# Reordering conv-out's seven products, metering the convolution's work, and beginning the first FFN in another order, in a two-layer decoder kernel

## The chip, the cores and the metric

One core of one Trainium2 chip runs the whole program. The metric is device time in microseconds (us), the median of several runs. TensorE is PE in the profile, VectorE DVE, ScalarE ACT, GpSimd POOL and SyncE SP.

## What is computed

The reference is a decoder of two layers in fp32, with D = 1024, S = 1024 tokens and d_ff = 2816. Layer 0 mixes tokens by a short gated convolution, layer 1 by dilated attention. Each mixer and each FFN is added to a residual stream behind an RMSNorm, and a last norm ends it:

```python
def short_conv_mixer(h, w_in, conv_k, w_out):
    b, c, u = jnp.split(h @ w_in, 3, axis=-1)
    y = lax.conv_general_dilated(c * u, conv_k[:, None, :], window_strides=(1,),
        padding=[(CONV_WIDTH - 1, 0)], dimension_numbers=("NWC", "WIO", "NWC"),
        feature_group_count=D_MODEL)          # depthwise, causal, width 3
    return (b * y) @ w_out
# x = x + mixer(rms_norm(x));  x = x + (silu(h @ w_gate) * (h @ w_up)) @ w_down, h = rms_norm(x)
```

## The kernel before

**Products.** Activations lie transposed: 8 tiles X[n] of 128 features by 1024 tokens, used as two halves of 512 columns. Each fp32 matrix product is made of three fp32r matmuls, since each operand is split into a high part (ACT, L159 for weights, L605 for moving operands) and a low part, the rest (DVE, L160 and L606). On top of that, `Strassen` multiplies 2x2 blocks with Winograd's seven products, numbered 1 to 7. Some take a difference or sum of weight blocks (the `combo` tiles, L227) or of moving blocks (t2, t3, `sums`). A whole product is twelve matmuls of 128x512: four tiles of the inner dimension, for each high by high (L613), high by low (L614) and low by high (L615). Its result is accumulated in one of 8 PSUM banks, used in rotation. The results of one bank are copied by ACT (`save`, L619) or added by DVE (`add`, L623).

**Order.** All instructions are written out in program order, each engine runs its own in that order, and waits follow from the data. `unit_order` gives the order of pairs (u, m) in a stage, where u is a unit (a pair of blocks of weight rows) and m the product. The weights of the coming products are loaded by SP into `raw` tiles and split ahead of use; how far ahead is set by tables (`upto`, `ahead`, AHEAD) and by calls of `ensure`. The hooks `start`, `filled` and `entry` are called behind each product and place everything else.

**The convolution layer.** `Conv` runs the in-projection in 12 units: unit u belongs to group q = u // 3, and u % 3 says whether its result is the c gate, the value or the b gate. For every result the generator `work` is put at the end of the list `waiting`. It multiplies c by the token's 1/rms (L1045), the value by c (L1049), runs the taps (`conv`: four instructions of 480, 32, 448 and 64 columns at L1034 and a multiply by 1/rms at L1035), multiplies by the b gate (L1057) and stores. `step(upto)` moves the list on by so much work: `idle` calls step(2) behind each product of the in-projection, `drain` calls step(4) or step(1) behind those of conv-out. `store` makes the differences that conv-out's products need (L787, L789) and sends all blocks to DRAM by POOL, except those of the last group, the `near` pair, that stay in SBUF.

**Conv-out.** `down` runs the products in the order DOWN = 1, 2, 6, 7, 4, 5, 3, each for four pairs k = 0, 2, 4, 6 of output tiles: 28 products. I write "product m of pair k". `feed` brings moving operands: SP loads blocks from DRAM (`hin`) and they are split; it is stepped behind products, and earlier at the products listed in CONV_FEED. Every product's result is copied or added into X (L858, L860), and the residual comes by an accumulating transfer from POOL (L850). The hook `entry` then squares finished halves of X for the FFN's norm (`chained`, L489: the third and fourth reach their sums by an accumulating transfer, later ones by DVE adds at L490), splits the sum of squares (ACT L516, DVE L520), sums over features by matmuls with ones (L528) and makes 1/rms with a logarithm and an exponential on ACT (L529, L530). The FFN's first eight moving operands are `first_half`: scale X (hcol, L1303), then split (L605, L606). The other column half comes in `second_half`, from tiles that `gained` made (ACT, and an accumulating transfer).

**First FFN and attention.** The FFN (`Swiglu`, stage key 0) starts with the products (0,1), (1,1), (0,2), (1,2), (2,1). Behind the first of them, `start(0)` runs `last_step` and the second half's statistics. In the attention layer, `QueryKey.mix` makes the operands of its first products (`differences`, L983 and L984) and has the statistics' copies and low parts made in the hook behind product (1,2), their ones-matmuls behind (3,1).

Of the kernel before, what the change touches and what calls it, by code (L numbers as in the profile page):

```python
# [13 lines left out]
ALU = mybir.AluOpType  # L14
# [101 lines left out]
def trunk(ctx: ExitStack, tc: tile.TileContext, x, gains_in, cwi, ck, cwo, wqkv, wo, relb,  # L116
# [103 lines left out]
    def add_pair(u, rows, w, eng, upto, low=(), sub=ALU.subtract):  # L220
# [13 lines left out]
        def summed(m):  # L234
            if m not in t:
                if m == 7:
                    t[7] = combo(raw(7, 0, 0), raw(7, 1, 0), sub)
                elif m == 3:
                    t[3] = combo(raw(3, 0, 1), t[6], sub)
                else:  # L240
                    t[5] = combo(raw(6, 1, 0), raw(6, 1, 1), ALU.add)
                    t[6] = combo(t[5], raw(6, 0, 0), sub)
            return t[m]

        def part(m):
            if m in (1, 2, 4):
                src = raw(m, *{1: (0, 0), 2: (0, 1), 4: (1, 1)}[m])
            else:
                src = summed(m) if m == 6 else (summed(m), t.pop(m))[0]
# [3 lines left out]
        sums_of.update({("m", u, m): lambda m=m: summed(m) for m in (6, 7, 3)})  # L253
# [44 lines left out]
    def unit_order(nu, conv):  # L298

        order = [(0, 1), (1, 1), (0, 2), (1, 2), (2, 1), (2, 2), (3, 1)]  # L300
# [3 lines left out]
        else:  # L304
            order += [(3, 2)] + [(u, m) for m in (6, 7, 4, 5) for u in (0, 1)]
            order += [(2, 6), (0, 3), (1, 3), (2, 5), (2, 7)]
            order += [(3, 6), (2, 4), (2, 3), (3, 5), (3, 7), (4, 1), (3, 4), (3, 3)]
# [7 lines left out]
        u = nu - 1  # L315
        return order[:-1] + [(u, 6), (u, 5), (u, 7), (u - 1, 3), (u, 4), (u, 3)]

    def add_units(key, nu, column):

        early = key in (CONV, QK)  # L320
        units, slabs, base = [], {}, len(raw_src)
        raw_base[key] = base
        for u in range(nu):
            if early:

                rows = ((0, 1), (2, 6), (3, 7, 8), (4, 9, 10), (5, 11, 12))[u] if u < 5 else (2 * u + 3, 2 * u + 4)
            else:
                rows = ((0, 1), (2, 5), (3, 6), (4, 7))[u] if u < 4 else (2 * u, 2 * u + 1)
            for n in range(len(rows)):
                slabs[rows[n]] = column(u, n % 2)  # L330
            if early:
# [3 lines left out]
                ahead.update({m: 6 if u < 5 else 2 * u + 6 for m in (1, 2)})  # L335
            elif u < 4:
# [14 lines left out]
            if not early and u > 4 and u % 2:  # L351
                add_deep(units[u], key, u, [[base + r - 2 * (1 - v) for r in rows] for v in range(2)],
                         lambda i, u=u: base + 2 * u + {1: 1, 2: 1, 3: 3, 4: 3}.get(i, 2))
        raw_src.extend(slabs[r] for r in range(len(slabs)))
        ops.extend(units[u][m] for u, m in unit_order(nu, early))
# [5 lines left out]
    def add_down(i, w):  # L361

        at = 0
        for c, qs in enumerate(chunks[CONV] if i == CONV else laid):
# [5 lines left out]
            upto = lambda m, r, u: r + {1: 4 + u, 2: 7, 5: 8 + u, 3: 11}.get(m, 7)  # L370
            units = [add_pair((i, c, 2 * u), (r + u, r + 4 + u), span, nc.vector,
                              lambda m, r=r, u=u: upto(m, r, u), sub=ALU.add) for u in range(4)]
# [1765 lines left out]
```

## Time and profile before

| | us |
|---|---|
| median of 3 runs (2090.3 to 2091.05) | 2090.67 |
| the profiled execution | 2091.3 |
| its span | 2089.5 |
| PE busy | 2066.4 |
| DVE busy | 1780.6 |
| ACT busy | 1052.9 |
| POOL busy | 283.9 |

The profiled execution took 1.8 us more than its span, and 0.6 more than the median. Times in rows are from the start of the span. A row of a timeline gives the start, the length, engine, line, operation, tiles out<-in, their shapes, and in brackets the idle time before it with what ended it. A row of the waits gives the waiter, what it waited for, the microseconds in total, how often, and the longest. A row of the windows gives a stretch and its length, busy time and count of each engine, the mean granted clock of PE (1.00 is full), and the share and rate of the DMA engines. In-projection ends at 242.29, conv-out at 328.94. A matmul's shown length is modelled and overlaps the next; matmuls are counted by their pitch, from start to start.

### The profile page before, as it was taken

Reading aid. Unit: us, or ns where it says so; the run is one execution under the profiler, and the core shown is the slowest. Engines: PE = TensorE matmul, PEld = TensorE weight load, DVE = VectorE, ACT = ScalarE, POOL = GpSimd, SP = SyncE. Lnnn points to the kernel's source line nnn. Section 1 sums busy time; section 2 is a strip of 40 time slices with the busy share of each in tenths; the row PEclk is TensorE's granted clock in tenths of the full one; section 3 lists DMA queues with packets and bytes.
Section 4 is the critical chain, followed back from the end, with each engine's and each line's share of the span. In section 5 each row is a group of like instructions: output and inputs, shape, how many; then the busy total and the mean of one; then the engine's idle time right before and its main releaser. Section 6 shows DMA issues by size and latency. Waiting matters only on the chain.

```text
span 2089.5 us, 30878 instructions
## 1 busy us (share of the span) xinstructions
PE 2066.4 (99%) x10906; PEld 1779.3 (85%) x10906; DVE 1780.6 (85%) x3318; ACT 1052.9 (50%) x1978; POOL 283.9 (14%) x398
## 2 busy tenths in 40 slices
PE   9999999999999999999999999999999999999998
PEld 7888787888888888887889999998888888888887
DVE  8898979988888888798985888988998888887896
ACT  7433466444443454456544666665544434455443
POOL 1000111110110111010223333311011001002000
PEclk9999999999999999999999999999999999999999
DMA  7223573233233488543656867955222333368532
GB/s 220 98 96 106 172 206 81 101 104 99 106 104 109 148 245 216 177 114 128 225 194 200 213 166 216 247 180 154 71 95 103 107 103 109 111 204 230 161 101 81
DMA packets 136201, 308.31 MB, mean 148 GB/s; under 512 B 15868, under 2 KB 46670, under 8 KB 136048
## 3 DMA queue, kind: packets, MB, share of 16 engines
q1 hardware_dynamic: 96272, 201.67, 31.9%
q0 software_dynamic: 32144, 89.98, 14.6%
q10 hardware_dynamic: 7632, 14.70, 1.9%
q8 instruction: 86, 1.41, 0.3%
q14 instruction: 67, 0.55, 0.1%
HBM read 211.30 MB, written 85.81 MB: 142 GB/s over the span
## 4 chain that ended last, share of the span: by engine, by line
PE 52%; DVE 1%; ACT 0%; issue 0%; DVEq 0%
PE bank L615 10%; PE bank L613 10%; PE bank L614 10%; PE bank L1732 5%; PE bank L415 2%; PE bank L417 2%; PE bank L416 2%; PE bank L1601 2%; PE bank L1603 1%; PE bank L1602 1%; PE bank L708 1%; PE bank L707 1%; PE bank L705 1%; PE bank L1658 1%; PE bank L1657 1%; DVE x L2047 0%
## 5 line engine op out<-in xcount | busy, mean ns | idle before, releaser
L614 PE MATMUL bank<-b,w 128*128 128x512 f32 x2176 | 850.2, 391 | 7.8 <-DVE b L606 7.5
L613 PE MATMUL bank<-b,w 128*128 128x512 f32 x2176 | 849.8, 391 | 1.8 <-ACT w L159 1.8
L615 PE MATMUL bank<-b,w 128*128 128x512 f32 x2176 | 849.4, 390 | 1.8 <-DVE w L160 1.7
L614 PEld LDWEIGHTS bank<-b,w 128*128 128x128 f32 x2176 | 409.8, 188 | 94.0 <-DVE b L606 9.6
L615 PEld LDWEIGHTS bank<-b,w 128*128 128x128 f32 x2176 | 409.7, 188 | 89.3 <-DVE w L160 4.2
L613 PEld LDWEIGHTS bank<-b,w 128*128 128x128 f32 x2176 | 410.1, 188 | 87.1 <-ACT w L159 2.5
L159 ACT ACTIVATE w<-combo 128x512 fp32r<-128x512 f32 (+2 forms) x512 | 268.9, 551 | 281.0 <-DVE combo L227 239.7
L160 DVE TENSOR_TENSOR w<-combo,w 128x512 fp32r<-128x512 f32 (+2 forms) x512 | 297.7, 594 | 34.2 <-ACT w L159 33.6
L619 ACT ACTIVATE part<-bank 128x512 f32<-128x512 f32 x192 | 114.5, 596 | 390.3 <-PE bank L615 388.3
L160 DVE TENSOR_TENSOR w<-raw,w 128x512 fp32r<-128x512 f32 (+2 forms) x336 | 188.4, 581 | 39.5 <-ACT w L159 39.3
L623 DVE TENSOR_TENSOR part<-part,bank 128x256 f32<-128x256 f32 (+1 forms) x372 | 175.2, 500 | 30.7 <-PE bank L615 18.2
L159 ACT ACTIVATE w<-raw 128x512 fp32r<-128x512 f32 (+2 forms) x336 | 169.2, 535 | 16.7 <-PE bank L708 10.5
L860 DVE TENSOR_TENSOR x<-x,bank 128x512 f32<-128x512 f32 x152 | 103.9, 683 | 31.4 <-PE bank L615 30.4
L606 DVE TENSOR_TENSOR b<-hin,b 128x512 fp32r<-128x512 f32 x161 | 109.6, 686 | 22.1 <-ACT b L605 22.1
L227 DVE TENSOR_TENSOR combo<-raw 128x512 f32<-128x512 f32 (+1 forms) x184 | 121.7, 662 | 0.0
L605 ACT ACTIVATE b<-hin 128x512 fp32r<-128x512 f32 x161 | 98.7, 619 | 8.4 <-DMA hin<-part 4.9
L708 PE MATMUL bank<-b,w 128*128 128x256 f32 x288 | 81.5, 283 | 0.0
L707 PE MATMUL bank<-b,w 128*128 128x256 f32 x288 | 81.5, 283 | 0.0
L705 PE MATMUL bank<-b,w 128*128 128x256 f32 x288 | 81.3, 282 | 0.0
L415 PE MATMUL bank<-w_hi,w 128*128 128x512 f32 (+1 forms) x208 | 76.5, 368 | 0.0
L417 PE MATMUL bank<-w_hi,w 128*128 128x512 f32 (+1 forms) x208 | 74.4, 358 | 0.0
L416 PE MATMUL bank<-w_lo,w 128*128 128x512 f32 (+1 forms) x208 | 74.4, 358 | 0.0
(242 smaller groups left out, 3231.9 us busy)
## 6 DMA issues: line engine op xcount, KB each, us to landing
hin<-part SPq DMA_DIRECT2D x140, 256.0 KB, 4.6
raw<-in_ffn_w_gate SPq DMA_DIRECT2D x44, 512.0 KB, 3.7
raw<-in_ffn_w_up SPq DMA_DIRECT2D x44, 512.0 KB, 3.6
part<-sum POOLq DMA_DIRECT2D x80, 256.0 KB, 2.3
raw<-in_attn_w_qkv SPq DMA_DIRECT2D x27, 512.0 KB, 4.7
raw<-in_conv_w_in SPq DMA_DIRECT2D x24, 512.0 KB, 3.6
raw<-in_ffn_w_down SPq DMA_DIRECT2D x32, 384.0 KB, 6.1
part<-part POOLq DMA_DIRECT2D x40, 256.0 KB, 2.5
```

Of the source, the lines that this page charges most:

```text
L159: nc.scalar.activation(hi, src, AF.Copy)
L160: low = lambda: eng.tensor_tensor(out=lo, in0=src, in1=hi, op=ALU.subtract)
L227: eng.tensor_tensor(out=c, in0=a, in1=b, op=op)
L415: nc.tensor.matmul(b, whi[:, a], ahi[:, s], start=first, stop=False)
L416: nc.tensor.matmul(b, whi[:, a], alo[:, s], start=False, stop=False)
L417: nc.tensor.matmul(b, wlo[:, a], ahi[:, s], start=False, stop=last)
L606: return lambda: eng.tensor_tensor(out=lo, in0=t, in1=hi, op=ALU.subtract)
L613: nc.tensor.matmul(b, hi[:, a], bhi, start=start and k == 0, stop=False, skip_group_check=True)
L614: nc.tensor.matmul(b, hi[:, a], blo, start=False, stop=False, skip_group_check=True)
L615: nc.tensor.matmul(b, lo[:, a], bhi, start=False, stop=k == n - 1, skip_group_check=True)
L619: nc.scalar.activation(t, b, AF.Copy)
L623: nc.vector.tensor_tensor(out=t, in0=t, in1=b, op=ALU.add)
```

## The change

It has four parts.

1. **Conv-out.** The products run in the order 1, 5, 6, 3, 7, 4, 2, and the two column halves change roles (`cols(h)` is the other half, and the b-gated blocks are stored as (t, 1 − h)). Products 5 and 6 share a weight sum, made at 5 (`five_first`). Unit 11 of the in-projection ends in the order 5, 6, 3, 7, 4, behind (10,3) and (10,4); its product 5 is saved by ACT. The near pair's differences are made as soon as both of their blocks are there (`store_near`). Weights are taken less far ahead at first (AHEAD), and `feed` is stepped by a table (CONV_STEPS) ahead of `drain`.
2. **Convolution work.** `step` adds its allowance (2.5 behind a product of the in-projection, 1.5 behind one of conv-out) to a credit of at most 5, and work goes on while credit is left. Ahead of conv-out, the last (0, 1) result's work goes to the head of the list.
3. **First FFN.** Product (2,1) comes third instead of fifth, (4,1) ahead of (0,6) instead of ahead of (3,4), with new places for their weights. The hook `entry` is timed anew for the new order. Behind the FFN's first product `last_step` makes the second half's sum of squares and its split ahead of the rest of the first half's operands; in both FFNs. In the second column half of the convolution layer a third square goes by transfer.
4. **Attention's statistics.** Their copies and low parts are made behind the first product, ahead of the differences, and their ones-matmuls still behind (3,1).

```diff
+CONV_DOWN = (1, 5, 6, 3, 7, 4, 2)
-AHEAD, AHEAD_TO = (7, 7, 7, 8, 11, 11, 11), 31
-CONV_FEED = {(11, 7): 2, (11, 4): 1, (11, 3): 1}
+AHEAD, AHEAD_TO = (4, 5, 6, 8, 9, 11, 11), 31
+CONV_FEED = {(11, 5): 1, (11, 6): 1, (11, 3): 1, (11, 7): 1}
+CONV_STEPS = (2, 1, 1, 0), (2, 2, 0, 0)
+PACE = 2.5, 1.5
...
+                elif five_first:
+                    if 5 not in t:
+                        t[5] = combo(raw(5, 1, 0), raw(5, 1, 1), ALU.add)
+                    if m == 6:
+                        t[6] = combo(t.pop(5), raw(6, 0, 0), sub)
...
-        order = [(0, 1), (1, 1), (0, 2), (1, 2), (2, 1), (2, 2), (3, 1)]
+        order = [(0, 1), (1, 1)] + ([(2, 1), (0, 2), (1, 2)] if key == 0 else [(0, 2), (1, 2), (2, 1)]) + [(2, 2), (3, 1)]
...
-            order += [(3, 2)] + [(u, m) for m in (6, 7, 4, 5) for u in (0, 1)]
+            order += [(3, 2)] + [(4, 1)] * (key == 0) + [(u, m) for m in (6, 7, 4, 5) for u in (0, 1)]
...
+        if nu > QK_PAIRS:
+            return order[:-2] + [(u - 1, 3), (u - 1, 4)] + [(u, m) for m in (5, 6, 3, 7, 4)]
         return order[:-1] + [(u, 6), (u, 5), (u, 7), (u - 1, 3), (u, 4), (u, 3)]
...
-            if k in (2, 3):
+            by_transfer = (2, 3, 4) if c0 and not late else (2, 3)
+            if k in by_transfer:
                 nc.gpsimd.dma_start(out=(acc, self.odd)[k % 2], in_=to, accum_op=ALU.add)
...
+            if self.key == CONV and u == self.nu - 1 and m == 5:
+                d["five"] = self.save(d["r"])
...
+            cols = lambda h: half(1 - h if one else h)
...
-                    self.drain(c, m, k)
                     if k // 2 in steps:
-                        for _ in range(1 + (one and i == 2)):
+                        for _ in range(CONV_STEPS[i > 1][k // 2] if one else 1):
                             next(feed, None)
+                    self.drain(c, m, k)
...
-                for _ in self.store(q, c, y):
-                    yield 0
+                c = t, 1 - h
+                for _ in self.store_near(c, y) if q == self.near else self.store(q, c, y):
+                    yield 1
...
-            while self.waiting and (upto is None or upto > 0):
+            self.credit = min(self.credit + upto, 5)
+            while self.waiting and self.credit > 0:
                 cost = next(self.waiting[0], None)
...
-                self.step(2)
+                self.step(PACE[0])
...
-                self.step(4 if m == 1 else 1)
+            self.step(PACE[1])
...
             def start(n):
                 if n == 0:
                     ensure(self.at(2, 2))
+                    next(stats)
+                    next(stats)
                     next(prep)
...
-                    last_step()
-                    for m in (6, 7):
-                        next(stats)
-                        if not self.key:
-                            combos[0, 1](m)
+                    last_step(stats)
...
-            if m not in (2, 4, 5, 3):
+            if m not in (3, 7, 4, 2):
                 return
-            n, h, at = k + (m in (4, 5)), int(m in (5, 3)), j + 4 * (m in (4, 3))
+            n, h, at = k + (m in (7, 4)), int(m in (4, 2)), j + 4 * (m in (7, 2))
...
-        def last_step():
+        def last_step(stats):
+            norm.flush()
+            next(stats)
             run(pre[0])
-            norm.flush()
+            next(stats)
+            for t in () if i else (7, 6):
+                sw.gained(t)
```

How it moves instructions, at three places on DVE. In the rows, L606 and L628 are the low part of a moving operand `b`, L160 and L163 that of a weight, L227 and L230 a weight combination, L1057 and L1106 the b gate's multiply, L789, L787 and L842 the near pair's differences.

The first place is the start of conv-out. DVE before, the last rows up to b_2397, which is the last operand of product 2:

```order
L1057 TENSOR_TENSOR y_2268<-y_2268,part_2117 128x512
L606 TENSOR_TENSOR b_2341<-hin_2188,b_2341 128x512
L227 TENSOR_TENSOR combo_2345<-raw_2157 128x512
L227 TENSOR_TENSOR combo_2347<-combo_2345,raw_2126 128x512
L160 TENSOR_TENSOR w_2349<-combo_2315,w_2349 128x512
L789 TENSOR_TENSOR sums_2337<-y_2196,y_2268 128x512
L606 TENSOR_TENSOR b_2370<-hin_2239,b_2370 128x512
L227 TENSOR_TENSOR combo_2374<-raw_2198 128x512
L227 TENSOR_TENSOR combo_2376<-combo_2374,raw_2128 128x512
L160 TENSOR_TENSOR w_2378<-combo_2347,w_2378 128x512
L787 SCALAR_TENSOR_TENSOR sums_2337<-sums_2337,y_2028 128x512
L606 TENSOR_TENSOR b_2397<-y_2123,b_2397 128x512
```

DVE now, from part_2170, the add that waits for the third-last product of the in-projection, as part_1977 does before (L623, 39 instructions up to and with b_2397):

```order
L645 TENSOR_TENSOR part_2170<-part_2170,bank_2120 128x512
L628 TENSOR_TENSOR b_2206<-hin_2142,b_2206 128x512
L1106 TENSOR_TENSOR y_2118<-y_2118,part_2170 128x512
L842 TENSOR_TENSOR sums_2077<-y_2118,y_1953 128x512
L163 TENSOR_TENSOR w_2218<-raw_2177,w_2218 128x512
L645 TENSOR_TENSOR part_2233<-part_2233,part_2136 128x512
L628 TENSOR_TENSOR b_2236<-y_2118,b_2236 128x512
```

The difference sums_2077 and the last operand of product 1 (b_2236) now follow that add at once. The last operand of the second product, which is now 5, is b_2362<-sums_2077 and the 31st instruction from part_2170 on, two tap groups among them.

The second place is the first FFN's start, the rows up to the last operand of its first half. DVE before:

```order
L860 TENSOR_TENSOR x_2393<-x_2393,bank_2895 128x512
L490 TENSOR_TENSOR acc_2425<-acc_2425,sq_2992 128x512
L160 TENSOR_TENSOR w_3031<-raw_2690,w_3031 128x512
L606 TENSOR_TENSOR b_3007<-hcol_3005,b_3007 128x512
L490 TENSOR_TENSOR acc_2425<-acc_2425,sq_3027 128x512
L227 TENSOR_TENSOR combo_3074<-raw_2868 128x512
L227 TENSOR_TENSOR combo_3076<-combo_3074,raw_2688 128x512
L520 TENSOR_TENSOR sum_3072<-acc_2425,sum_3071 128x512
```

And now:

```order
L908 TENSOR_TENSOR x_2384<-x_2384,bank_3019 128x512
L510 TENSOR_TENSOR acc_2627<-acc_2627,sq_3013 128x512
L510 TENSOR_TENSOR acc_2627<-acc_2627,sq_3033 128x512
L1358 SCALAR_TENSOR_TENSOR hcol_3074<-x_2279,gains_68,rstd_2628 128x512
L628 TENSOR_TENSOR b_2993<-hcol_2991,b_2993 128x512
L628 TENSOR_TENSOR b_3076<-hcol_3074,b_3076 128x512
L541 TENSOR_TENSOR sum_3072<-acc_2627,sum_3071 128x512
```

Both adds of squares now come ahead of the last two operands, and the sum's low part directly behind them; two weight combinations are gone from between. From the add of conv-out's product 7 of pair 2 to b_3076 there are 56 instructions, and the add that waits for the third transferred square is the 49th.

The third place is the attention layer's statistics (sum, L520 and L541). DVE before:

```order
L983 SCALAR_TENSOR_TENSOR t3_9094<-x_7433,gains_68,t3_9094 128x512
L984 SCALAR_TENSOR_TENSOR t2_9098<-x_7395,gains_68,t3_9094 128x512
L606 TENSOR_TENSOR b_9132<-t2_9097,b_9132 128x512
L606 TENSOR_TENSOR b_9137<-t2_9098,b_9137 128x512
L623 TENSOR_TENSOR part_9083<-part_9083,bank_9141 128x512
L520 TENSOR_TENSOR sum_9169<-acc_8452,sum_9168 128x512
L520 TENSOR_TENSOR sum_9172<-acc_8452,sum_9171 128x512
```

And now:

```order
L1235 TENSOR_TENSOR acc_8454<-acc_8454,sq_9065 128x512
L163 TENSOR_TENSOR w_9087<-raw_8857,w_9087 128x512
L163 TENSOR_TENSOR w_9090<-raw_8857,w_9090 128x512
L541 TENSOR_TENSOR sum_9094<-acc_8454,sum_9093 128x512
L541 TENSOR_TENSOR sum_9097<-acc_8454,sum_9096 128x512
L1031 SCALAR_TENSOR_TENSOR t3_9101<-x_7181,gains_68,t3_9101 128x512
L1032 SCALAR_TENSOR_TENSOR t2_9105<-x_7142,gains_68,t3_9101 128x512
```

The two low parts have moved from behind the differences to ahead of them.

More of the change, by code (lines that the diff above doesn't have):

```diff
@@ L669, in whole @@
                 self.out(u, (0, 1), self.add(d.pop("u2"), d.pop("r")))
+            elif m == 7 and "five" in d:
+                self.out(u, (1, 1), self.add(d.pop("u3"), d.pop("five")))
             elif m in (5, 7) and "u3" in d and "r" in d:
@@ L780, in store @@
             t = {}
-            two = [page("sums") for _ in range(2)] if q == self.near else []
             def make(m, a, b, less=False):
-                t[m] = two[m in (5, 4)][:, half(m in (6, 5))] if two else half_page("sum")
+                t[m] = half_page("sum")
                 if less:
@@ L799, in store, with store_near @@
             make(5, b11, b12)
+        def store_near(self, c, g):
+            q = self.near
+            if not self.quads:
+                self.sums = [page("sums") for _ in range(2)]
+            self.quads[c] = g
+            if c != (0, 1):
+                self.put(q, {(0, 0): 1, (1, 0): 2, (1, 1): 3}[c], g)
+            for m, x, y in ((5, (0, 0), (0, 1)), (7, (1, 1), (0, 1)), (6, 7, (0, 0)), (4, 6, (1, 0))):
+                if m in self.quads or x not in self.quads or y not in self.quads:
+                    continue
+                yield
+                a, b = self.quads[x], self.quads[y]
+                t = self.quads[m] = self.sums[m in (6, 4)][:, half(m in (5, 4))]
+                if m in (6, 4):
+                    nc.vector.scalar_tensor_tensor(t, a, -1.0, b, op0=ALU.mult, op1=ALU.subtract)
+                else:
+                    nc.vector.tensor_tensor(out=t, in0=a, in1=b, op=ALU.subtract)
+                self.put(q, m, t)
+            if 4 in self.quads:
+                self.quads, self.sums = {}, None
         def put(self, q, m, t):
@@ L1050, in work @@
                 yield 1
+                yield 0
                 if h == 0:
@@ L1132, in start @@
                     self.ahead = 3
-                elif n > len(self.order) - 10 and n % 2:
-                    self.ahead += 1
+                elif n == len(self.order) - 4:
+                    self.ahead = 4
             def gather():
@@ L1253, in gather, with spread @@
                 self.first(0)
-                next(stats)
-                next(stats)
+            def spread():
+                run(stats)
                 self.first(1)
-            def spread():
                 self.first(2)
+                next(prep)
                 ensure(self.at(1, 6))
```

120 lines of the change are left out of this document (68 added, 52 removed).

## The prediction

> **What bounds the kernel now.** I read the page first, then the waits of the matmul engine, then windows over the places where they fall, then the timelines of PE, DVE and ACT there.
>
> ```profile
> PE 2066.4 (99%) x10906; PEld 1779.3 (85%) x10906; DVE 1780.6 (85%) x3318; ACT 1052.9 (50%) x1978; POOL 283.9 (14%) x398
> ```
>
> PE is busy 99% of the span, so only what PE loses can be won. The change adds and removes no matmul. What PE waits for, over the span:
>
> ```profile
> PE bank L614 <- DVE b L606: 7.5, 5, 2.2
> PE bank L528 <- DVE sum L520: 1.9, 3, 0.9
> PE bank L613 <- ACT w L159: 1.8, 2, 1.6
> PE bank L615 <- DVE w L160: 1.7, 3, 0.7
> PE bank L528 <- ACT sum L516: 1.1, 2, 0.6
> ```
>
> The largest sum is the wait for the low part of a moving operand, written by DVE (L606). The windows are an undisturbed stretch of conv-out, its start, the stretch around the first-half statistics, the start of the first FFN, and the attention layer's statistics:
>
> ```profile
> core 0: us, PE busy (x) PEld busy (x) DVE busy (x) ACT busy (x) POOL busy (x), PEclk, DMA share, GB/s
> 272.75:305.39 32.64, 32.64 (x146) 27.03 (x144) 23.68 (x38) 22.35 (x42) 8.12 (x10) 1.00 0.97 264
> 242.29:272.75 30.46, 24.52 (x98) 18.84 (x96) 29.26 (x50) 13.58 (x27) 4.03 (x5) 0.94 0.46 102
> 305.39:318.06 12.67, 11.89 (x51) 9.31 (x50) 11.27 (x18) 5.12 (x9) 0.00 (x0) 1.00 0.25 95
> 328.94:345.56 16.62, 13.76 (x51) 10.36 (x50) 14.85 (x25) 11.86 (x22) 3.50 (x4) 0.90 0.46 95
> 973.67:984.79 11.12, 10.07 (x42) 7.20 (x40) 10.93 (x19) 9.70 (x18) 0.00 (x0) 1.00 0.00 0
> ```
>
> The first row is the yardstick: 144 weight loads in 32.64 us, 0.2267 us a matmul, 2.72 us a product of twelve. (The weight loads count the matmuls; the counts beside PE take in those that straddle an edge.) The others then have too much time: 30.46 − 96 × 0.2267 = **8.70**; 12.67 − 50 × 0.2267 = **1.33**; 16.62 − 50 × 0.2267 = **5.28**; 11.12 − 40 × 0.2267 = **2.05**. Together 17.4 us lie in the places that the change rearranges. These are PE's delays there (242.29 is conv-out's first product, 256.31 product 2 of its first pair):
>
> ```profile
> 242.29 0.39 PE L613 MATMUL bank<-b,w 128*128 128x512 f32 x1
> 244.56 0.50 PE L614 MATMUL bank<-b,w 128*128 128x512 f32 x1 [0.51 <-DVE b L606]
> 247.56 0.50 PE L614 MATMUL bank<-b,w 128*128 128x512 f32 x1 [2.04 <-DVE b L606]
> 256.31 0.39 PE L613 MATMUL bank<-b,w 128*128 128x512 f32 x1
> 262.40 0.50 PE L614 MATMUL bank<-b,w 128*128 128x512 f32 x1 [2.17 <-DVE b L606]
> 338.37 0.50 PE L614 MATMUL bank<-b,w 128*128 128x512 f32 x1 [1.56 <-DVE b L606]
> 340.90 0.50 PE L528 MATMUL bank<-sum,ones_r 128*128 128x512 f32 x1 [0.77 <-DVE sum L520]
> 977.64 1.10 PE L528 MATMUL bank<-sum,ones_r 128*128 128x512 f32 x3 [0.86 <-DVE sum L520]
> ```
>
> A wait is paid twice where the clock drops behind it:
>
> ```profile
> 256.00:267.00 11.00, 7.62 (x26) 5.50 (x25) 10.49 (x18) 4.45 (x8) 0.90 (x2) 0.84 0.53 106
> 340.00:346.00 6.00, 5.24 (x16) 4.06 (x16) 5.96 (x11) 3.61 (x8) 0.00 (x0) 0.72 0.53 89
> ```
>
> The share of the clock that is missing is work lost: 1.00 − 0.84 = 0.16 of 11.00 us is 1.8 us, 0.28 of 6.00 us is 1.7 us. These 3.5 us are inside the 8.70 and the 5.28. By the Trainium skill, "TensorE: Matmul & The Clock Gate", section "Why this matters for your kernels", a gap must exceed some 3 us to bring the slow clock; the trace does not agree, as single waits of 2.2 and 1.6 us stand ahead of the two drops. By that rule the drops would have another cause and could stay, which is a rival below.
>
> **Term A: the start of conv-out (8.70).** DVE works in order, and before, what PE wants next stands behind convolution work:
>
> ```profile
> 233.18 0.69 DVE L160 TENSOR_TENSOR w<-raw,w 128x512 fp32r<-128x512 f32 x1 [1.55 <-ACT w L159]
> 239.71 0.68 DVE L623 TENSOR_TENSOR part<-part,bank 128x512 f32<-128x512 f32 x1
> 240.31 0.71 DVE L1034 SCALAR_TENSOR_TENSOR y<-part,taps,y 128x480 f32<-128x480 f32 x1
> 242.00 0.69 DVE L1035 TENSOR_TENSOR y<-y,rstd 128x512 f32<-128x512 f32 x1
> 242.61 1.29 DVE L160 TENSOR_TENSOR w<-raw,w 128x512 fp32r<-128x512 f32 x2
> 246.82 0.68 DVE L606 TENSOR_TENSOR b<-y,b 128x512 fp32r<-128x512 f32 x1
> 261.67 0.69 DVE L606 TENSOR_TENSOR b<-y,b 128x512 fp32r<-128x512 f32 x1
> ```
>
> From start to start, a whole 128x512 operation takes 0.605 us (239.71 to 240.31, 242.00 to 242.61), the four instructions of one conv tap group 1.69 (240.31 to 242.00). Before, from the add at 239.71 to the last operand of product 2 (261.67, b_2397 in the order) there are 39 instructions: two tap groups and 31 whole ones, 3.4 + 18.8 = 22.1 us; 239.71 + 22.1 = 261.8 against 261.67 seen, so counting works. PE began that product at 256.31 and wanted its fourth tile ten matmuls later at 258.58; the operand is complete about 3.8 late. DVE itself was also late: the add at 239.71 needs the third-last product of the in-projection, which ends two products (5.44 us) ahead of conv-out at 242.29, so at 236.85; it ran 2.7 us behind that and the 0.2 from a matmul to its reader, 1.55 of it the wait at 233.18.
>
> After, the last unit ends in another order, and product 5 comes second, whose fourth tile is the sum sums_2077, made 27 instructions sooner. From the add that waits for the same point (part_2170) to that last operand (b_2362) I count 31 instructions, 2 tap groups and 23 whole ones: 3.4 + 13.9 = 17.3 us. DVE should be in time for that add: ahead of it stand 12 whole operations and one tap group, 8.95 us, that can begin when the sixth-last product ends, at 242.29 − 6 × 2.72 = 225.97 and 0.2 for the reader; they are done at 235.1, 1.7 ahead of 236.85. With 0.2 from matmul to add and 0.3 for a copy by ACT of the product before, the operand arrives at 236.85 + 0.2 + 17.3 + 0.3 = 254.65. PE wants it at 242.29 + 4 × 2.72 + 10 × 0.2267 = 255.44: 0.8 early. Product 6 needs 17 more instructions, 10.3 us: 264.9 against 266.3. Ends: nothing lost, or DVE late again by 2.7 us, a wait of 1.9 and a clock drop of 1.7, 3.6 in all. I take **0.5**, the size of the row at 244.56, since 0.8 is a small margin: gain 8.2. The same rows carry the metering of conv work: it only spreads the same multiplies and taps. The extra operations on POOL and SP (loads of the parts, weights in new order) I price at nothing: the DMA share at this start is 0.46, where the undisturbed stretch ran at 0.97 without a loss; if that cover failed it would be a wait like Term A's upper end.
>
> **Term B: first-half statistics (1.33).** DVE, to the end of conv-out and into the FFN:
>
> ```profile
> 314.24 0.69 DVE L520 TENSOR_TENSOR sum<-acc,sum 128x512 fp32r<-128x512 f32 x1 [1.22 <-ACT sum L516]
> 320.00 1.41 DVE L1303 SCALAR_TENSOR_TENSOR hcol<-x,gains,rstd 128x512 f32<-128x512 f32 x2 [1.05 <-ACT rstd L530]
> 322.06 0.68 DVE L860 TENSOR_TENSOR x<-x,bank 128x512 f32<-128x512 f32 x1
> 331.37 0.69 DVE L160 TENSOR_TENSOR w<-raw,w 128x512 fp32r<-128x512 f32 x1 [0.44 <-ACT w L159]
> 334.51 0.68 DVE L860 TENSOR_TENSOR x<-x,bank 128x512 f32<-128x512 f32 x1
> 337.02 0.69 DVE L160 TENSOR_TENSOR w<-raw,w 128x512 fp32r<-128x512 f32 x1 [1.22 <-ACT w L159]
> 337.63 0.68 DVE L606 TENSOR_TENSOR b<-hcol,b 128x512 fp32r<-128x512 f32 x1
> ```
>
> The sum's low part (314.24) waited for ACT and PE for it. After, copy and low part are issued behind the last product 7, and the matmuls that use them behind the third product 4, three products or 8.16 us on. Ends 0 and 1.33; I take the whole, since the wait seen (1.22) is far under 8.16.
>
> **Term C: first FFN (5.28).** Unit 0's product 2 needs all of the second four operands. Before, it starts 5.44 us after the FFN's first product (at 328.94, the edge of that window); after, product 1 of unit 2 stands between, 8.16 us. After, the FFN begins at 242.29 + 28 × 2.72 + 0.46 = 318.9, and its fourth tile is wanted at 318.9 + 8.16 + 2.27 = 329.3. DVE, from the add behind conv-out's product 7 of pair 2 (end at about 291.3) to the last operand, has 56 instructions, 34.4 us with their tap-free mean of 0.61: 325.9. Spare 3.4. A new wait comes in: in the second half a third square now reaches its sum by an accumulating transfer, and DVE's next add into that sum (L510) waits for it, with the operands above queued behind.
>
> ```profile
> acc<-sq POOLq DMA_DIRECT2D x4, 256.0 KB, 5.6
> ```
>
> It is issued behind the add after product 2 of pair 0 (38th of the 56, 314.4) and a square, lands at 314.4 + 0.6 + 0.6 + 5.6 = 321.2, and the add is the 49th, at 320.6: 0.6 of the 3.4. Before, the stretch held the waits for ACT 1.22, 1.05, 0.44 and 1.22 above, 3.9 us. If all come back PE waits 1.1; so Term C keeps between 0 and 1.1 of its loss by these rows, and all of it if they double. Beginning unit 4 sooner puts one more product ahead of the second half's operands, and squares first shorten the way to the second statistics (wait 0.77 at 340.90); the two gain sweeps moved behind conv-out add two copies on ACT (0.6 each) and two transfers on POOL there, for operands wanted products later. I take the whole 5.28.
>
> **Term D: attention's statistics (2.05).**
>
> ```profile
> 976.91 1.29 DVE L520 TENSOR_TENSOR sum<-acc,sum 128x512 fp32r<-128x512 f32 x2
> 977.68 0.60 ACT L619 ACTIVATE part<-bank 128x512 f32<-128x512 f32 x1
> 982.30 0.68 ACT L529 ACTIVATE rstd<-bank,eps 128x512 f32<-128x512 f32 x1
> ```
>
> The sums' low parts run at 976.91, behind 14 operations for the first differences, and PE wanted them at 976.39. After, they stand ahead of these, 14 × 0.62 = 8.7 us sooner. What is late next: the product behind the statistics takes the bank whose logarithm ACT must first read (0.68, as at 982.30), and ACT first copies the product before (0.60 as at 977.68). PE is ready at 976.39 + 4 × 0.23 = 977.3 and ACT done at about 976.6 + 0.5 + 0.7 = 977.8: 0.5 lost. Ends: 2.05 gained, or nothing, if that logarithm is also behind a copy as long as before. I take **1.5**.
>
> **Sum.** 8.2 + 1.33 + 5.28 + 1.5 = 16.3 us. The profiled execution took 2091.3: 2091.3 − 16.3 = 2075.0. The median of the runs is 0.6 lower, so 2074.4. About 0.2%, 4.2 us, is what a measurement of this kernel can tell from no change.
>
> **Rivals.**
>
> - *DVE late again at conv-out.* The lateness of 2.7 us (239.71) recurs against a margin of 0.8; wait and clock drop cost 3.6, 3.1 more than I took: 2077.5. For it: 1.55 of that lateness was a wait for ACT, which the new order does not remove by name. Against it: more than the margin is needed. 14%.
> - *The FFN's start still waits.* If DVE waits there for ACT and that transfer 8 us instead of the 4.5 allowed for, or the statistics come late again, up to all of the 5.28 stays: 2079.7. Against: three products' length instead of two. 10%.
> - *The clock drops are not caused by the waits.* Then 3.5 us stay: 2077.9. Against: each drop stands right behind a wait, and the window 242.29 to 272.75 has 0.94 only by the one in it. 5%. This is what the Trainium skill's rule on gaps, named above, would make of the time.
> - *Slower: the metered work blocks DVE.* With a credit instead of fixed steps, the multiply that reads the bank of the product just issued can come to stand ahead of the splits that PE needs next; DVE then waits for that product's end, 2.72 us, and passes it on to PE where less than that is in hand (1.7 us at the place worked out above). If it came at each of the seven units 5 to 11, 7 × 2.72 = 19.0 us, more than the whole gain: 2074.4 + 19.0 = 2093.4. For it: at part_2170 DVE, by the count above, stands 1.7 us ahead of the product that it waits for. Against: Term A has that wait in it and PE loses nothing by it, since operands then in work are for products further on. 4%.
> - *Several of these together*, or part of the last: within 0.2%, 5%.
>
> My forecast keeps 62%. Faster 0.14 + 0.10 + 0.05 + 0.62 = 0.91; same 0.05; slower 0.04. Range: the low end is all 17.4 us gained and 0.6 for the median, 2073.3, and 0.4 below it for the spread of the runs (2090.3 to 2091.05): 2072.9. The high end takes in the first three rivals and the first two in part together: 2082.
>
> **What would show it.** In the changed profile: no wait by the low split of operands over 1 us between conv-out's first and ninth product, and PEclk 1.00 there (A); the ones-matmuls beside products without a gap (B); no wait in the first FFN's product 2 of unit 0 or 1, PEclk 1.00 (C); the four ones-matmuls in the attention layer within about 1 us, and a wait for ACT of about 0.5 behind them (D). I am wrong if DVE has waits for PE's banks (L645 or its multiplies) within the in-projection that PE then repeats, or if the total falls by less than 10 us.

## The result and the profile after

The changed kernel takes **2076.71 us** (median of 4 runs, 2075.70 to 2077.46), the kernel before 2090.56 beside it: 13.9 us less, a ratio of 0.9933 with a 95% interval of 0.9916 to 0.9950. The forecast was 2074.4, with a range of 2072.9 to 2082.0. The profiled execution took 2077.46, its span 2075.7.

Windows of the changed kernel over the places that lost time before: all of conv-out; the first FFN's start (six products, where the window before had four); the attention layer's statistics (the same 40 matmuls as before). Then two where PE has new losses, and the first 18 products of the program:

```profile
core 0: us, PE busy (x) PEld busy (x) DVE busy (x) ACT busy (x) POOL busy (x), PEclk, DMA share, GB/s
244.14:320.81 76.67, 76.67 (x340) 63.46 (x339) 73.00 (x122) 49.33 (x90) 14.72 (x17) 1.00 0.76 198
320.81:337.62 16.81, 16.81 (x76) 13.89 (x75) 16.01 (x26) 15.10 (x27) 3.48 (x4) 1.00 0.53 115
961.27:971.09 9.82, 9.42 (x42) 7.46 (x41) 9.52 (x16) 7.33 (x14) 1.49 (x2) 1.00 0.00 0
237.72:244.14 6.42, 5.73 (x26) 4.43 (x25) 6.39 (x12) 4.10 (x11) 0.00 (x0) 1.00 0.45 172
392.02:398.51 6.49, 5.75 (x26) 4.43 (x25) 5.92 (x13) 2.33 (x5) 0.54 (x1) 1.00 0.11 40
5.64:62.68 57.04, 52.39 (x217) 41.37 (x218) 50.68 (x80) 41.59 (x67) 5.17 (x6) 0.97 0.73 209
```

The row of the kernel before that answers to the last one:

```profile
5.64:61.82 56.18, 53.02 (x218) 41.79 (x218) 50.69 (x80) 41.54 (x67) 5.17 (x6) 0.97 0.74 213
```

PE is busy in the whole of conv-out and of the FFN's start, at full clock: the 8.70, 1.33 and 5.28 us are gone. At attention's statistics 9.82 − 36 × 0.2267 − 4 × 0.23 = 0.74 of 2.05 is left. Two losses are new: 6.42 − 5.44 = 0.98 at the end of the in-projection, 6.49 − 5.44 = 1.05 late in the first FFN. The program's start took 0.86 longer. Sum: 17.36 − 0.74 − 0.98 − 1.05 − 0.86 = 13.7, against 2089.5 − 2075.7 = 13.8 between the spans.

The start is not touched by the change: in its 18 products PE lost 6.0 to 8.1 us in the profiled executions of this study, whichever the kernel. So about 1 us in any total is chance, and the verdicts on single waits below go by the waits themselves.

PE's waits in the changed kernel, and the rows of the three that the change brought:

```profile
PE bank L637 <- DVE w L163: 2.0, 3, 0.9
PE bank L635 <- ACT b L996: 1.6, 2, 1.0
PE bank L635 <- ACT w L162: 1.6, 1, 1.6
PE bank L635 <- ACT part L641: 1.4, 2, 0.7
```

```profile
241.25 0.50 PE L635 MATMUL bank<-b,w 128*128 128x512 f32 x1 [0.69 <-ACT part L641]
395.60 0.50 PE L635 MATMUL bank<-b,w 128*128 128x512 f32 x1 [0.74 <-ACT part L641]
965.48 0.50 PE L635 MATMUL bank<-b,w 128*128 128x512 f32 x1 [0.40 <-ACT rstd L550]
```

No wait for a moving operand's low part (DVE b L628) is left. In its place stand two for a copy by ACT (L641): product 7 of a unit ends, ACT has to read its bank, and product 4, which adds to the same bank, is now next in the order. In the old order one other product lay between.

The places on DVE and ACT on which the forecast rested:

```profile
233.59 0.69 DVE L628 TENSOR_TENSOR b<-hin,b 128x512 fp32r<-128x512 f32 x1 [2.93 <-ACT b L627]
239.52 0.68 DVE L645 TENSOR_TENSOR part<-part,bank 128x512 f32<-128x512 f32 x1
256.30 0.68 DVE L628 TENSOR_TENSOR b<-sums,b 128x512 fp32r<-128x512 f32 x1
328.57 0.69 DVE L628 TENSOR_TENSOR b<-hcol,b 128x512 fp32r<-128x512 f32 x1 [0.17 <-ACT b L627]
```

```profile
232.44 0.60 ACT L641 ACTIVATE part<-bank 128x512 f32<-128x512 f32 x1 [2.50 <-PE bank L637]
240.60 0.60 ACT L641 ACTIVATE part<-bank 128x512 f32<-128x512 f32 x1 [1.39 <-PE bank L637]
964.74 0.68 ACT L550 ACTIVATE rstd<-bank,eps 128x512 f32<-128x512 f32 x1
```

At 233.59 DVE has stood still 2.93 us for the high part of an operand, which ACT makes only behind a copy (232.44) that itself waits for PE. Product 5's last operand is done at 256.30 + 0.68 = 256.98. Conv-out starts at 244.14 here, so it is wanted at 244.14 + 10.88 + 2.27 = 257.29: 0.3 in hand. The FFN's (0,2) starts at 328.97 and wants its fourth tile at 331.24; the operand is done at 329.26, 2.0 ahead.

### The profile page after: what moved, and what is told of

Its sections match the earlier page's. It is cut to its first block, busy times and chain, and to the rows that moved or that the text cites. A ratio compares the mean times of both kernels' runs of the same rounds, so it can differ in the third digit from the quotient of the medians.

```text
span 2075.7 us, 30885 instructions
## 1 busy us (share of the span) xinstructions
PE 2059.1 (99%) x10906; PEld 1776.7 (86%) x10906; DVE 1780.7 (86%) x3317; ACT 1053.5 (51%) x1979; POOL 284.8 (14%) x399
## 4 chain that ended last, share of the span: by engine, by line
PE 97%; DVE 1%; DMA 1%; ACT 0%; issue 0%; SPq 0%; DVEq 0%; ACTq 0%
PE bank L635 23%; PE bank L637 23%; PE bank L636 23%; PE bank L1791 5%; PE bank L731 3%; PE bank L734 3%; PE bank L733 3%; PE bank L435 2%; PE bank L437 2%; PE bank L436 2%; PE bank L1660 2%; PE bank L1662 1%; PE bank L1661 1%; PE bank L1717 1%; PE bank L1716 1%; DMA x<-in_x 1%
## 5 line engine op out<-in xcount | busy, mean ns | idle before, releaser
L163 DVE TENSOR_TENSOR w<-combo,w 128x512 fp32r<-128x512 f32 (+2 forms) x512 | 297.8, 594 | 32.5 <-ACT w L162 32.1
L641 ACT ACTIVATE part<-bank 128x512 f32<-128x512 f32 x193 | 115.1, 596 | 394.4 <-PE bank L637 387.1
L163 DVE TENSOR_TENSOR w<-raw,w 128x512 fp32r<-128x512 f32 (+2 forms) x336 | 188.3, 582 | 35.7 <-ACT w L162 35.3
L645 DVE TENSOR_TENSOR part<-part,bank 128x256 f32<-128x256 f32 (+1 forms) x371 | 174.7, 501 | 30.4 <-PE bank L637 19.5
L628 DVE TENSOR_TENSOR b<-hin,b 128x512 fp32r<-128x512 f32 x161 | 109.3, 686 | 18.4 <-ACT b L627 18.4
L230 DVE TENSOR_TENSOR combo<-raw 128x512 f32<-128x512 f32 (+1 forms) x184 | 121.8, 662 | 0.0
```

Source lines behind the costliest of these rows:

```text
L163: low = lambda: eng.tensor_tensor(out=lo, in0=src, in1=hi, op=ALU.subtract)
L230: eng.tensor_tensor(out=c, in0=a, in1=b, op=op)
L645: nc.vector.tensor_tensor(out=t, in0=t, in1=b, op=ALU.add)
```

## The experiments

All times are medians. "Slower" and "faster" without more is against the changed kernel at 2076.71. The changed kernel did not run beside the experiments; the kernel before did, with medians from 2089.82 to 2090.56 over the sessions, so differences under 1 us say little by themselves. A delay is taken from the start of a product to the start of the next, less 2.72; the brackets in rows count only idle time and read less.

**The first FFN's order undone.** Both moves: `(2,1)` fifth and `(4,1)` late again.

```diff
-([(2, 1), (0, 2), (1, 2)] if key == 0 else [(0, 2), (1, 2), (2, 1)])
+[(0, 2), (1, 2), (2, 1)]
-[(3, 2)] + [(4, 1)] * (key == 0) + ...   + [(4, 1)] * (key != 0) + [(3, 4), (3, 3)]
+[(3, 2)] + ...                           + [(4, 1), (3, 4), (3, 3)]
```

> The changed kernel with the first FFN's products in the old order again: (2,1) fifth and (4,1) between (3,7) and (3,4). In the changed kernel the last operand of unit 0's product 2 is ready at 329.26, and wanted 2.0 later. Theory (the extra product only adds cover that is mostly not needed, and (4,1) moved away costs a bank wait of 1.0): the FFN's product (0,2) then starts one product sooner, at 326.25, wants its fourth tile at 328.5 and waits about 0.7 with no clock drop; the wait of 1.0 at (3,4) goes: total within 1 us of the changed kernel, about -0.3. Rival (the early start of unit 2 is what removed the 5.3 us): the wait of before comes back with a clock drop, 3 to 5 us slower than the changed kernel.

2078.23, 1.5 slower. The first line is in (0,2), its third product; the second at the start of (0,3):

```profile
327.23 0.51 PE L636 MATMUL bank<-b,w 128*128 128x512 f32 x1 [0.89 <-DVE b L628]
368.78 0.47 PE L635 MATMUL bank<-b,w 128*128 128x512 f32 x1 [1.36 <-DVE part L645]
```

At (0,2) stand 1.3 us of delay, where Term C was 5.28. The wait at (3,4) is gone. A new one, 1.5 us of delay, came ahead of (0,3): it adds to the bank of the unit's product 5, which DVE has to read first (L645). So the early unit 2 is worth 1.3 of the 5.28. The rest of Term C does not need it: neither the waits at the second half's ones-matmuls nor the slow clock of before came back.

**Only (4,1) late again.** The second pair of lines above alone.

> The changed kernel with only product (4,1) of the first FFN back between (3,7) and (3,4). Theory: products 7 and 4 of a unit accumulate in the same bank, ACT has to copy the bank after 7 before 4 may write it, and (4,1) was the cover: the wait of 0.74 at (3,4) (1.03 us with what follows) goes, 1.0 us faster than the changed kernel, unless second-half operands, which end at 344.5, are late for (0,6), which then starts at 343.06 and wants its fourth tile at 345.3. Rival: (4,1) early covers a wait there, and the total is the same or slower.

2077.35, 0.6 slower, as the rival had it:

```profile
367.95 0.47 PE L635 MATMUL bank<-b,w 128*128 128x512 f32 x1 [1.70 <-DVE part L645]
```

The 1.05 at (3,4) is gone, and 1.9 of delay stand ahead of (0,3). The early (4,1) gives DVE one product more before that bank is wanted.

**Another product between 7 and 4.**

```diff
-order += [(3, 6), (2, 4), (2, 3), (3, 5), (3, 7)] + [(4, 1)] * (key != 0) + [(3, 4), (3, 3)]
+order += [(3, 6), (2, 4), (3, 5), (3, 7), (2, 3), (3, 4), (3, 3)] if key == 0 else ...
```

> The changed kernel with product (2,3) of the first FFN moved two places, to between (3,7) and (3,4); (4,1) stays early. Theory (bank copied by ACT between 7 and 4): the wait at (3,4) goes, 1.0 us faster than the changed kernel, and no new wait. Rival (ACT is late there for another reason, its queue): the wait stays or moves to the next product, no gain.

**2075.58** (2075.15 to 2075.76), 1.1 faster, as the theory had it; a row of its waits:

```profile
PE bank L635 <- ACT part L641: 0.7, 1, 0.7
```

One of the two waits for a copy is left, the in-projection's. This is the fastest kernel of the study, by its median.

**A bank of its own for product 4.** For the in-projection's last unit:

```diff
+own = m == 4 and "five" in d
-if m == 1:
+if m == 1 or own:
     d["p"] = self.bank()
...
+if own:
+    self.out(u, (1, 0), self.add(d.pop("u3"), d.pop("p")))
...
```

> The changed kernel with a PSUM bank of its own for product 4 of the in-projection's last unit, and one more DVE add (0.6 us) for its result. Theory (DVE is 1.6 us late at part_2170, and product 5 of conv-out has its last operand only 0.3 ahead of use): the wait of 0.69 at (11,4) goes (0.96 us with what follows), but conv-out starts that much sooner and PE then waits 1.0 to 1.3 at conv-out's first product 5: no gain, 0 to 0.4 us slower. Rival (the bank wait stands alone): 1.0 us faster.

2077.46, 0.8 slower. The wait at (11,4) is gone and this one is there, at conv-out's first product 5:

```profile
257.43 0.50 PE L636 MATMUL bank<-b,w 128*128 128x512 f32 x1 [1.21 <-DVE b L628]
```

Its delay is 1.5 us. The theory holds: the 0.98 lost ahead of conv-out costs nothing by itself, as DVE is no earlier.

**Attention's statistics back behind the differences.**

```diff
 def start(n):
     if n == 0:
...
-        next(stats)
-        next(stats)
...
 def gather():
...
+    next(stats)
+    next(stats)
...
```

> The changed kernel with the attention layer's statistics back behind product (1,2), behind the differences. Theory: the wait of 0.86 us at the ones-matmuls comes back, 1.7 to 2.0 us slower than the changed kernel, all of it there. Rival (DVE comes to that place less late now, since everything ahead of it is sooner): under 0.5 us.

2078.22, 1.5 slower.

```profile
964.02 1.10 PE L549 MATMUL bank<-sum,ones_r 128*128 128x512 f32 x3 [0.85 <-DVE sum L541]
```

The wait of before (0.86) is back, equal to 0.01. In the changed kernel 2.05 − 0.74 = 1.3 us are won there.

**Metering undone.** The changed kernel, with the convolution work stepped by 2, 4 and 1 as before and no credit. The new costs and stops in the work list stay, and so does the loop that empties the list as far as the last (0, 1) result needs.

```diff
-self.credit = min(self.credit + upto, 5)
-while self.waiting and self.credit > 0:
+while self.waiting and (upto is None or upto > 0):
...
-self.step(PACE[0])
+self.step(2)
-self.step(PACE[1])
+if self.waiting:
+    self.step(4 if m == 1 else 1)
```

> The changed kernel with the convolution work stepped as before (2 behind a product of the in-projection, 4 or 1 behind one of conv-out, no credit). Theory (the reordering alone shortens the way to product 5's operands, metering only spreads the same work): within 1 us of the changed kernel. Rival (metering is what keeps DVE in time): work piles up at conv-out's start and PE waits there 2 us or more, with a clock drop, 4 to 8 us slower.

2087.36, **10.7 slower**: the rival holds, and by more than it asked. PE, then ACT, then the window behind:

```profile
247.63 0.79 PE L635 MATMUL bank<-b,w 128*128 128x512 f32 x1 [7.93 <-ACT part L641]
```

```profile
245.10 0.25 ACT L1068 ACTIVATE pad<-part 128x62 f32<-128x62 f32 x1 [6.15 <-DVE part L1097]
...
247.00 0.57 ACT L641 ACTIVATE part<-bank 128x512 f32<-128x512 f32 x1
```

```profile
248.00:254.00 6.00, 6.00 (x16) 4.65 (x16) 6.00 (x11) 2.42 (x6) 0.00 (x0) 0.54 0.94 339
```

Without the credit, convolution work is left over when the last (0, 1) result asks for its y at once. The rest of the list is then emitted in one go, ahead of the copy of product 7's bank. ACT stands 6.15 us at the first step that needs DVE (the pad), the copy comes at 247.00, and product 4 starts 8.1 us late, at 0.54 of the clock. With the slow clock and the smaller waits behind it, 12.2 us are lost from there to conv-out's product 6, where the kernel before lost 8.7. The new order without metering is worse there than the old order. Whether the smaller allowance (2 for 2.5, with a store step that now costs 1) or the missing credit leaves the work over was not tried apart.

**Own bank, and operands fed one product sooner.**

```diff
-CONV_FEED = {(11, 5): 1, (11, 6): 1, (11, 3): 1, (11, 7): 1}
+CONV_FEED = {(10, 4): 1, (11, 5): 1, (11, 6): 1, (11, 7): 1}
```

> The changed kernel with the own bank for product (11,4) and the loads and splits of conv-out's operands stepped one product sooner each up to the last ((10,4), (11,5), (11,6), then (11,7)), so that DVE does not wait 2.93 us for the first of them. Theory: DVE reaches part_2170 in time, so the own bank's gain holds, 0.9 us faster than the changed kernel. Rival: DVE waits as long further on, since ACT's copy or the load is the limit: no gain.

2077.26, 0.6 slower, and 0.72 of wait at product 5: mostly as the rival had it.

```profile
232.42 0.60 ACT L641 ACTIVATE part<-bank 128x512 f32<-128x512 f32 x1 [2.50 <-PE bank L637]
232.92 0.62 ACT L627 ACTIVATE b<-hin 128x512 fp32r<-128x512 f32 x1
```

```profile
233.57 0.69 DVE L628 TENSOR_TENSOR b<-hin,b 128x512 fp32r<-128x512 f32 x1 [2.77 <-ACT b L627]
```

The first operand came sooner, but the second stands on ACT behind a copy that waits for PE, and DVE behind it: 2.77 instead of 2.93. Here the place of the split in ACT's order decides, not when its data land.

**Four more DVE operations.** They leave every value as it is.

```diff
+elif n == len(self.order) - 2:
+    t = norm.acc[:, half(0)]
+    for _ in range(4):
+        nc.vector.tensor_tensor(out=t, in0=t, in1=t, op=ALU.max)
```

> The changed kernel with four more whole DVE operations (2.4 us, they leave every value as it is) ahead of the last operand of conv-out's first product. Theory (the count of DVE operations up to an operand sets PE's wait; 0.3 us are in hand at product 5 and 0.1 at product 1): PE waits 2.1 us at the first product 5, in all 2 us slower, or 3.8 if the clock drops behind it as it did in the kernel before. Rival (DVE has slack that the count does not see): under 1 us.

2078.67, 2.0 slower. The first line is at conv-out's product 1, the second at product 5; the window is the second's:

```profile
245.15 0.50 PE L636 MATMUL bank<-b,w 128*128 128x512 f32 x1 [0.24 <-DVE b L628]
258.20 0.50 PE L636 MATMUL bank<-b,w 128*128 128x512 f32 x1 [1.44 <-DVE b L628]
```

```profile
254.00:262.00 8.00, 6.43 (x28) 4.66 (x27) 7.97 (x14) 3.47 (x7) 1.71 (x2) 1.00 0.78 138
```

The delays are 0.5 and 2.1 us: 2.6, where the four operations take 2.4. The count of DVE operations up to an operand is what PE waits by here. The clock stayed full.

**Metering alone, on the kernel before.** First the credit, in the old order of products:

```diff
+self.credit = min(self.credit + upto, 5)
-while self.waiting and (upto is None or upto > 0):
+while self.waiting and self.credit > 0:
...
-self.step(2)
+self.step(2.5)
-self.step(4 if m == 1 else 1)
+self.step(1.5)
```

> The kernel before with one thing of the change: the convolution work stepped by the credit (2.5, 1.5, at most 5). Order of products as before. Counted in DVE's order, from the add that waits for the third-last product of the in-projection to the last operand of conv-out's product 2 there are now 31 whole operations and one tap group, 20.4 us, against 22.1 and a late start. Theory (metering moved convolution work ahead of the end of the in-projection, and that is most of the gain at conv-out's start): waits there of about 0.2 at product 1, none at product 2, about 0.9 at product 6, no clock drop: 7 to 8 us faster than the kernel before. Rival (the gain is the new order's): the waits at products 1 and 2 stay, with the clock drop, under 2 us faster.

2093.93 against 2089.82 for the kernel before beside it, a ratio of 1.0017 (1.0008 to 1.0026): slower. My theory of this run fell. In the profiled execution PE lost 3.1 us within the in-projection, behind its first 18 products, where the kernel before lost nothing, 2.1 less at conv-out's start, and 1.1 more at the first FFN's, where the same waits had a longer stretch of slow clock behind them. A row within the in-projection, and one at conv-out's product 1:

```profile
99.11 0.51 PE L615 MATMUL bank<-b,w 128*128 128x512 f32 x1 [0.98 <-DVE w L160]
251.27 0.50 PE L614 MATMUL bank<-b,w 128*128 128x512 f32 x1 [3.74 <-DVE b L606]
```

Then also the change's two other edits of the work list: a stop ahead of the taps (which the section on the change does not name), and a cost of 1 instead of 0 for a step of the store:

```diff
     nc.vector.tensor_tensor(out=g, in0=g, in1=v, op=ALU.mult)
     yield 1
+    yield 0
...
     for _ in self.store(q, c, y):
-        yield 0
+        yield 1
```

> The kernel before with all of the change's metering: the credit, and the two costs in the work list that the run with the credit alone left out (a stop behind the value's multiply, ahead of the taps, and a store step costs 1). Order of products as before. In DVE's order the taps now stand behind weight splits that they preceded in that run. Counted from the add that waits for the third-last product of the in-projection: 9 whole operations to the last operand of conv-out's product 1, done 2 us ahead of use; 31 and one tap group to that of product 2, 1 us ahead; 50 and one tap group to that of product 6, 2.7 us late. Theory (the stop is what keeps taps out of the way of weight splits, and metering then gives most of the gain at conv-out's start): no waits within the in-projection, at conv-out's start only 2.7 at product 6, 5 to 6 us faster than the kernel before, less what the first FFN's start takes back, whose wait can only grow. Rival (the new order is needed as well, for DVE is late by more than the count): waits of 3 us or more at products 1 or 2 of conv-out, no faster than the kernel before.

2089.94 against 2090.06, 0.9998 (0.9989 to 1.0008): no difference, as the rival had it. The waits for weights within the in-projection are gone. The two edits together do that; that it is the stop is my theory, not shown. At conv-out's product 2 stands a delay of 5.1 us, in two gaps, and a clock of 0.51 behind it. DVE and PE there:

```profile
231.03 0.69 DVE L160 TENSOR_TENSOR w<-raw,w 128x512 fp32r<-128x512 f32 x1 [2.03 <-DMA hin<-part_conv]
239.86 0.68 DVE L623 TENSOR_TENSOR part<-part,bank 128x512 f32<-128x512 f32 x1
260.23 0.68 DVE L606 TENSOR_TENSOR b<-y,b 128x512 fp32r<-128x512 f32 x1
```

```profile
257.11 0.50 PE L614 MATMUL bank<-b,w 128*128 128x512 f32 x1 [1.21 <-DVE b L606]
260.97 0.80 PE L614 MATMUL bank<-b,w 128*128 128x512 f32 x1 [2.88 <-DVE b L606]
```

The product that the add waits for ends at 236.98; DVE is 2.7 us behind that and its 0.2, just as before, though by another wait: 2.03 at 231.03, by the profile for the load of an operand, where the kernel before had 1.55 for ACT. From there the count holds: 260.23 + 0.68 − 239.86 = 21.05 us, where I had counted 20.4. So all of the metering in the old order gains next to nothing at this place (PE still loses 8.3 us there, against 8.7), and the new order without the credit loses more than before; together they gain all of the 8.7.

**Both bank waits and the way to product 5.** (2,3) between, the own bank, and weights split fewer products ahead.

```diff
-AHEAD, AHEAD_TO = (4, 5, 6, 8, 9, 11, 11), 31
+AHEAD, AHEAD_TO = (2, 4, 5, 8, 9, 11, 11), 31
```

> The changed kernel with (2,3) between (3,7) and (3,4), the own bank for product (11,4), and conv-out's weights split 2, 4 and 5 products ahead at its first three products instead of 4, 5 and 6, which takes four whole operations (2.4 us) from ahead of product 5's last operand. Theory (count of operations): the wait of 1.2 at product 5 that the own bank alone brought is gone, and both bank waits: 2.0 us faster than the changed kernel, 1.0 faster than with (2,3) alone. Rival: a weight is late instead, or DVE is late further on; no faster than with (2,3) alone.

2075.76: as fast as (2,3) alone, not 1 faster. The delay at product 5 fell from 1.5 to 0.3, so 0.7 were won at this place. This came up, in the FFN's product (0,4):

```profile
355.97 0.50 PE L637 MATMUL bank<-b,w 128*128 128x512 f32 x1 [0.49 <-DVE w L163]
```

With its neighbours it is a delay of 1.0. DVE waits for nothing between 330 and 372 us there; PE came sooner and met it.

**Squares last again.** `norm.flush()` and the statistics behind `run(pre[0])`.

> The changed kernel with the second half's last square and sum behind the rest of the first half's operands again. In DVE's order one add moves from ahead of the last operand of the FFN's second four to behind it, so that operand comes 0.6 sooner and the sum's low part at the same place. Theory (2.0 us are in hand at that operand and 1.8 at the sum): the same time as the changed kernel within 0.5 us. Rival (it is what removed the wait at the second half's ones-matmuls): 1 us or more slower.

2077.99, 1.3 slower; the theory fell. DVE waits at the sum, and PE 28 us later, at (0,4):

```profile
329.20 0.69 DVE L541 TENSOR_TENSOR sum<-acc,sum 128x512 fp32r<-128x512 f32 x1 [0.75 <-ACT sum L537]
```

```profile
357.29 0.50 PE L637 MATMUL bank<-b,w 128*128 128x512 f32 x1 [0.45 <-DVE w L163]
```

The spare at the two operands was there, as I had counted, but DVE's lost time was not given back before (1,6), (0,7), (0,4) and (0,3); PE's delays are 0.3, 0.2, 0.75 and 0.1 about there, in all 1.3.

## Why the prediction was right, and where it was wrong

The time fell within the range, 2.3 us above the forecast, since the four places cleared as they were forecast to. Their sum was 16.3 and 13.9 came: two waits that were not forecast (2.0) and a longer start of the program in the profiled execution (0.9, chance) are most of the difference.

- **Term A**: forecast 8.2, measured 8.7 at conv-out itself, 7.7 with the 0.98 that is now lost just ahead of it. The count of operations was right where it was tried (four more cost what they take), and the spare at product 5 was 0.3 against 0.8 forecast. But two steps in it failed. I had DVE at the add 1.7 us early; it came at 239.52, 1.6 behind the product that ends at 237.72 and the 0.2. My count let it run without a wait, and it had stood 2.93 at 233.59 for ACT. And PE, 0.98 late itself, hid that, which was luck: with PE in time the wait was there (own bank, 1.5).
- **"Metering only spreads the same multiplies and taps"**, priced at nothing, was the step that failed worst: without the credit and its allowance the same kernel loses 10.7 us. The sum held all the same, since I counted instructions in an order that metering had already made. The same work in the same engine is not the same, if it is left over at the end, where it is emitted ahead of the copy and the splits that PE needs.
- **Two bank waits were missed**, 0.98 and 1.05. I followed operands and DVE through the new orders and not the bank that products 7 and 4 share. Term C's "Beginning unit 4 sooner puts one more product ahead of the second half's operands" names the good side of that move (1.9, as undoing it showed) and not that it took away the cover of the copy.
- **Term B** was as forecast. **Term C** came in full, and DVE was in time with 2.0 in hand (3.4 less the transfer's 0.6 forecast); the transfer itself made DVE wait for nothing that its rows show. But of the reasons given, the third product ahead is worth 1.3 of it, and squares first is worth 1.3 further down. What the other 4.0 came from was not tried apart. The rows show that the last operand is done 8.45 us behind the FFN's start (329.26 − 320.81), where it took 9.37 before (338.31 − 328.94), 0.9 sooner, and that the waits at the second statistics are gone; what made them go is only argued. And 1.7 of the 5.28 was slow clock, which the same waits need not bring (the last section).
- **Term D**: 1.5 forecast, 1.3 measured, with the wait that takes its place where it was put, 0.40 behind ACT's logarithm.
- **The clock**: the rival that the drops have another cause is out, since with the waits no drop is left in conv-out and the FFN. By products, PE was 3.9 late at the bracketed 2.17 (6.66 − 2.72, from 256.31), but in two gaps, 1.4 at 259.27 and 2.3 at 262.40, with two matmuls between. By the rule of the Trainium skill, "TensorE: Matmul & The Clock Gate", section "Why this matters for your kernels", it takes a gap of some 3 us to bring the slow clock. Single gaps in these runs agree with it: 1.4, 1.9 and 2.2 us left the clock alone, 3.9 and 8.1 did not. Neither drop named in the prediction has such a gap ahead of it, so there the trace still does not agree.
- **The range's rivals**: DVE late again at conv-out happened in part, hidden by PE's own delay; none of the others came. The slower one, metered work ahead of the splits that PE needs, did not come in the changed kernel, where taking the metering out did the harm; it did come in the old order with the credit alone, as 3.1 us within the in-projection.

## What to carry to other kernels

When products change their order, follow four things to each new neighbour: the moving operand, the weight, the bank and whoever must read the bank first. Two accumulations into one bank with a copy between them want another product between them. And where the engine that makes operands is nearly full (DVE was busy 73.00 of 76.67 us of conv-out), a saving ahead of it moves the wait to the next place at which that engine is late, unless operations are taken off its way.

## What the runs showed of the hardware

A gap is here the time from one matmul's start to the next one's, less 0.23. Single gaps of 1.4 (own bank, 257.43), 1.9 (only (4,1) late, 367.95) and 2.2 us (metering undone, 59.38) left the granted clock at 1.00 in the windows behind them. So did two gaps in one product, 0.7 at 244.56 and 2.2 at 247.56, in the kernel before:

```profile
248.00:256.00 8.00, 8.00 (x37) 6.61 (x36) 7.90 (x16) 4.52 (x9) 2.60 (x3) 1.00 0.54 96
```

A single gap of 3.9 (the credit alone on the kernel before) was followed by 0.61, one of 8.1 (metering undone) by 0.54, and gaps of 1.4 and 3.05 in one product (credit and stops) by 0.51. The first and the last of these:

```profile
251.84:256.09 4.25, 4.25 (x13) 3.30 (x12) 4.18 (x7) 1.76 (x4) 0.90 (x1) 0.61 0.57 104
261.98:267.06 5.08, 5.08 (x13) 4.01 (x12) 3.23 (x6) 1.67 (x3) 0.00 (x0) 0.51 0.32 103
```

Short gaps close together came out both ways. At the first FFN's start the kernel before has three within 2.5 us, 1.7 at 338.37, 0.7 at 339.63 and 1.0 at 340.90, and 0.72 behind them from 340 to 346. The credit alone and the credit with the stops, on the same kernel, have the same three gaps, equal to within 0.05 us, and in all three runs they come at the same times to within 0.8 us. For these two runs the same window reads 0.54 and 1.00:

```profile
340.00:346.00 6.00, 5.13 (x12) 3.79 (x13) 5.93 (x11) 3.72 (x8) 0.17 (x1) 0.54 0.61 102
340.00:346.00 6.00, 5.35 (x23) 4.43 (x24) 5.96 (x10) 3.62 (x7) 0.00 (x0) 1.00 0.48 82
```

So the sizes of such gaps do not settle by themselves whether the clock drops; what else does stays open. No run shows a single gap between 2.2 and 3.9 us without another just ahead of it.
